# Seven-product FFN up stage: quarter weights formed seven products ahead from four raw tiles, and the down stage's operands in the token forms' space

## The chip, the cores and the metric

One core of one Trainium2 chip runs the whole kernel. The metric is the device time of one execution. The kernel before took 1296.34 us (median of three runs, 1295.82 to 1298.61).

PE is the matrix engine (TensorE), PEld its weight loads, DVE the vector engine, ACT the scalar engine, POOL GpSimd, and SP the engine whose queue issues all DMAs here. Each engine takes its instructions in a fixed order.

## The reference

A transformer block in fp32 on 1024 tokens of width 1024: adaLN modulation, a mixer (attention and a short convolution), a residual with layer norm, and then a convolutional FFN with a second residual and layer norm. The change lies in the FFN:

```
def conv_ffn(h, w_up, ffn_conv_w, ffn_conv_b, w_down):
    u = causal_dwconv(h @ w_up, ffn_conv_w, ffn_conv_b)   # w_up 1024 x 5632, 3 taps along the tokens
    g, val = jnp.split(u, 2, axis=-1)
    return (jax.nn.silu(g) * val) @ w_down                # w_down 2816 x 1024
...
x = layer_norm(DEEPNORM_ALPHA * x + gate_f * ff, ln2_g, ln2_b)
```

## The kernel before

**fp32 from three products.** Every operand is split into a rounded high part (a cast on ACT) and the remainder (a subtract on POOL or DVE). A product is hh + hl + lh, three matmuls of 128x128 by 128x512 each.

**Up stage.** The 2816 columns of each half of `w_up` make 22 pairs i, one gate tile and one value tile of 128 columns. Pairs 0 and 1 are computed plainly (`first_pairs`, L828), while the second half of the tokens is still being made. Pairs 2 to 21 are each a 2x2 block product by seven products (Winograd's form), so one pair takes 7 x 12 = 84 matmuls (`quarter_mm`, L930) where the plain form takes 96. I number a pair's products n = 0 to 6 by their weight quarter: a11, a12, a22, s2, s1, s3, s4. The token side (h2 and its sums T1 to T4) is formed once, by `hsum` (L903) and `hform` (L897, L898). The weight side is formed per pair: four combinations on DVE (L938 to L941) and seven splits `wquarter`, a cast on ACT (L923) and a subtract on POOL (L924). The split quarters go into a ring of eight tiles, `wform`: qb0h, qb0l, qb1h, qb1l, wf0 to wf3.

**Raw weights.** A pair reads two raw tiles of 512 KB (`load_raw`, L766), from a pool of two buffers, so the next pair's loads wait until this pair's quarters are formed.

**Evacuation.** Products land in PSUM (`pw`: two banks for the accumulating products and s3; `p`: p2, p4, p3), and are added up in SBUF tiles cg and cv by ACT copies and DVE adds (L951 to L967). Then come the taps (ACT L834, DVE L836), silu (ACT L860), the product (DVE L861), and a store of 512 KB to DRAM (`acts`, L862).

**Down stage.** Before it starts, the pools of the up stage are closed and new ones opened (L979 on). For each slice i the kernel loads acts[i] and w_down[i] (L1020, L1023), multiplies w_down by the gate row on POOL (L1024) and splits both (L126: casts on ACT; subtracts on DVE for acts, on POOL for w_down). Groups of 2, 4, 4, 4, 4, 4 slices run over eight token tiles, two halves each (L1036), and DVE adds each result to the residual y (L1040). The residual (x1s) is reloaded into y after the token forms have read it (L976).

**What sets the order.** A scheduler fixes each engine's order at build time, from data dependences and its own estimate of durations; the order of the text is only a priority.

```
    for i in range(2, NFF):
        up_pair(i)
        if 2 <= i < 2 + NT:
            SP.dma_start(out=ra[i - 2], in_=x1s[i - 2])
    close(tfp, wup, h2p)
    fp, fpool = pool_("fp", bufs=2)
```

Of the kernel before, what the change touches and what calls it, by code (L numbers as in the profile page):

```python
# [67 lines left out]
def block_kernel(ctx: ExitStack, tc: tile.TileContext, a: dict, out: bass.AP, dbg=None):  # L68
# [1048 lines left out]
```

## Time and profile before

| | us |
|---|---|
| median of the runs | 1296.34 |
| profiled execution, its own time | 1297.43 |
| its span in the trace | 1295.6 |
| PE busy | 1159.7 (90%) |
| DVE / POOL / ACT busy | 876.8 / 677.9 / 536.2 |
| first_pairs ends, seven-product pairs begin | 609.1 |
| last seven-product matmul ends | 1017.3 |
| down stage runs without gaps from | 1043.0 |
| last matmul | 1284 |

The trace's times count from the start of the span. A matmul's listed length (about 0.39 us) overlaps the next one's; the distance from start to start is its price.

### The profile page before, as it was taken

To read this page: it belongs to the slowest core of one execution; us is meant where nothing else is said; L and a number is where in the kernel's file an instruction comes from. 1 tells how busy PE (TensorE), PEld (TensorE's weight loads), DVE (VectorE), ACT (ScalarE), POOL (GpSimd) and SP (SyncE) were. 2 spreads that over 40 slices of the span, in tenths; PEclk is the share of its full clock that TensorE was granted. 3 is DMA by queue.
4 is the path that set the end of the run, shared out by engine and by line. 5 is a ranking of instruction groups with operands and counts; after the bars stand their busy time and mean duration, and the time that the engine had idled before them with its cause. 6 is when DMAs were issued, how large, how long until landed. Compare 5 with 4: busy or idle time off the path is not lost.

```text
span 1295.6 us, 14458 instructions
## 1 busy us (share of the span) xinstructions
PE 1159.7 (90%) x5204; PEld 934.1 (72%) x5204; DVE 876.8 (68%) x1207; ACT 536.2 (41%) x836; POOL 677.9 (52%) x434
## 2 busy tenths in 40 slices
PE   2998978879988989999899999999999389999996
PEld 1766756767867768877688877778778268888885
DVE  6964889867767647679577777777777573543347
ACT  2544323237768723447344444444444342221011
POOL 4666625313538623536655656556566098834226
PEclk9989988889989989999899999999999789999998
DMA  9301454643244133232322212222122364421002
GB/s 376 138 25 49 133 198 156 187 111 80 54 99 130 34 114 114 66 98 99 114 84 79 82 65 83 81 81 82 67 83 79 109 232 131 146 98 51 15 32 99
DMA packets 46219, 134.47 MB, mean 104 GB/s; under 512 B 5452, under 2 KB 15308, under 8 KB 45124
## 3 DMA queue, kind: packets, MB, share of 16 engines
q1 hardware_dynamic: 46148, 133.55, 32.0%
q8 instruction: 41, 0.67, 0.2%
q14 instruction: 30, 0.25, 0.1%
HBM read 100.76 MB, written 19.92 MB: 93 GB/s over the span
## 4 chain that ended last, share of the span: by engine, by line
PE 45%; POOL 16%; DMA 14%; DVE 14%; issue 6%; ACT 3%; SPq 1%; POOLq 0%; DVEq 0%; ACTq 0%
PE pd L1036 16%; DMA ur<-w_up_in 8%; PE pso L704 6%; POOL wf L924 6%; PE pw L930 5%; PE p L930 4%; PE s L594 3%; DMA y<-ada_r_in 3%; PE pu L828 2%; PE tp L628 2%; PE pa L283 2%; POOL qb1l L924 1%; POOL qb0h L924 1%; POOL qb1h L924 1%; POOL qb0l L924 1%
## 5 line engine op out<-in xcount | busy, mean ns | idle before, releaser
L924 POOL TENSOR_TENSOR wf<-ur,wf 128x512 fp32r<-128x512 f32 x68 | 114.0, 1692 | 84.1 <-ACT wf L923 84.1
L1040 DVE TENSOR_TENSOR y<-pd,y 128x512 f32<-128x512 f32 x96 | 61.6, 683 | 104.6 <-PE pd L1036 104.5
L930 PE MATMUL p<-h2h,wf 128*128 128x512 f32 x240 | 81.3, 400 | 3.8 <-POOL wf L924 3.3
L923 ACT CAST wf<-ur 128x512 fp32r<-128x512 f32 x68 | 41.0, 620 | 104.7 <-DMA ur<-w_up_in 76.5
L1024 POOL TENSOR_TENSOR rd<-rd,gate_f 128x1024 f32<-128x1024 f32 x22 | 58.4, 2664 | 49.2 <-DMA rd<-w_down_in 49.2
L283 PE MATMUL psc<-hTh,hwc 128*128 128x512 f32 x192 | 65.1, 407 | 14.7 <-DVE y L528 8.8
L283 PE MATMUL psc<-hTl,hwc 128*128 128x512 f32 x192 | 64.4, 402 | 0.0
L632 DVE TENSOR_TENSOR ptl<-tp,pth 128x512 fp32r<-128x512 f32 (+1 forms) x96 | 50.7, 550 | 20.1 <-ACT pth L631 19.4
L283 PE MATMUL psc<-hTh,lwc 128*128 128x512 f32 x192 | 63.7, 400 | 0.0
L1036 PE MATMUL pd<-h2h 128*128 128x512 f32 x144 | 40.7, 411 | 23.6 <-ACT h2h L123 21.2
L599 DVE TENSOR_REDUCE mx<-s 128x1 f32<-128x128 f32 (+3 forms) x64 | 47.6, 752 | 17.3 <-PE s L594 15.8
L930 PEld LDWEIGHTS p<-h2h,wf 128*128 128x128 f32 x240 | 44.9, 190 | 17.4 <-POOL wf L924 6.8
L283 PEld LDWEIGHTS psc<-hTh,hwc 128*128 128x128 f32 x192 | 37.4, 196 | 24.3 <-issue 11.3
L601 ACT ACTIVATE p<-s,mx 128x128 f32<-128x128 f32 (+3 forms) x64 | 47.8, 748 | 12.7 <-DVE mx L599 12.4
L631 ACT CAST pth<-tp 128x512 fp32r<-128x512 f32 (+1 forms) x96 | 43.7, 485 | 19.0 <-PE tp L628 17.1
L1036 PEld LDWEIGHTS pd<-h2h 128*128 128x128 f32 x144 | 28.4, 199 | 30.7 <-ACT h2h L123 21.6
L628 PE MATMUL tp<-ident,p 128*128 128x128 f32 x288 | 47.9, 276 | 0.7 <-DVE ptl L632 0.6
L930 PE MATMUL p<-h2l,wf 128*128 128x512 f32 x120 | 47.3, 394 | 0.0
L836 DVE SCALAR_TENSOR_TENSOR rbuf<-rbuf,cols,rbuf 128x1023 f32<-128x1023 f32 (+1 forms) x24 | 34.7, 1465 | 18.4 <-ACT rbuf L834 18.4
L283 PEld LDWEIGHTS psc<-hTl,hwc 128*128 128x128 f32 x192 | 37.9, 197 | 8.2
L283 PEld LDWEIGHTS psc<-hTh,lwc 128*128 128x128 f32 x192 | 37.4, 195 | 8.3
L836 DVE SCALAR_TENSOR_TENSOR rbuf<-cu,cols,rbuf 128x1023 f32<-128x1023 f32 (+1 forms) x24 | 37.8, 1593 | 6.7 <-ACT rbuf L834 6.7
(929 smaller groups left out, 3678.1 us busy)
## 6 DMA issues: line engine op xcount, KB each, us to landing
ur<-w_up_in SPq DMA_DIRECT2D x44, 512.0 KB
y<-ada_r_in SPq DMA_DIRECT2D x32, 512.0 KB
ra<-acts SPq DMA_DIRECT2D x22, 512.0 KB
rd<-w_down_in SPq DMA_DIRECT2D x22, 512.0 KB
ada<-ada_m_in SPq DMA_DIRECT2D x8, 1024.0 KB
acts<-rbuf SPq DMA_DIRECT2D x14, 512.0 KB
rwc<-w_conv_in SPq DMA_DIRECT2D x12, 512.0 KB
xn<-x_in SPq DMA_DIRECT2D x8, 512.0 KB
```

The source lines that it names most:

```text
L283: T.matmul(out=ps[hf][0:n_out, :], lhsT=w[:, k, :], rhs=hT[hf][m][:, k, :], start=first and i == 0, stop=last and i == 2)
L599: V.tensor_reduce(out=mx, in_=st[:, 0:n], op=ALU.max, axis=mybir.AxisListType.X, negate=True)
L601: A.activation(out=pt[:, 0:n], in_=st[:, 0:n], func=AF.Exp, bias=mx, accum_out=sm[:, c:c + 1])
L628: T.transpose(tp[:, q4 * P:(q4 + 1) * P], pts[q4][:, kt * P:(kt + 1) * P], ident)
L632: V.tensor_tensor(ptl[:, c0:], tp[:, c0:], f(pth[:, c0:]), op=ALU.subtract)
L704: T.matmul(out=ps[:, hf, :], lhsT=l[:, i, :], rhs=r[:, hf * 512:(hf + 1) * 512], start=part == 1 and i == 0 and n == 0, stop=part == 0 and ...
L836: V.scalar_tensor_tensor(out=u[:, d:n], in0=src[:, 0:n - d], scalar=w(2 - d), in1=u[:, d:n], op0=ALU.mult, op1=ALU.add)
L924: G.tensor_tensor(t[:, 1], s_, f(t[:, 0]), op=ALU.subtract)
L930: T.matmul(out=ps, lhsT=w[:, m, k, :], rhs=b[mb][:, k, :], start=first and k == 0 and n == 0, stop=k == 3 and n == 2, skip_group_check=True)
L1024: G.tensor_tensor(raw, raw, gate_f, op=ALU.mult)
L1036: T.matmul(out=ps[hf], lhsT=l[:, sl], rhs=r[:, hf * 512:(hf + 1) * 512], start=k == 0 and m == 0, stop=k == n - 1 and m == 2)
L1040: V.tensor_tensor(rs_, ps[hf], rs_, op=ALU.add)
```

## The change

Four parts. (1) Raw weights have four tiles: pair i+2 loads into the two that pair i used, as soon as its seventh quarter is formed; the same four tiles later hold acts and w_down. (2) The text forms quarter j+7 before product j. Pairs 2 and 3 start interleaved. (3) p2 and p4 go to single PSUM banks (`o`, `nm`), p4 is copied by ACT and product 3 added by DVE; the cg/cv/u tiles come from a list of five. The token forms are all subtracted on DVE; the gate row is made after pair 5. (4) The down stage's operands live in the tiles of the token forms and quarters, in the order in which pair 21's products free them; its first two slices are loaded and formed inside pair 21.

```
+    raws += [tfpool.tile([P, 1024], F32, name=f"wr{i}") for i in range(2, 4)]
...
-    hform(R[1][1], tforms[1], V)
-    hform(R[1][0], tforms[3], G)
-    hform(R[0][0], tforms[0], V)
-    hform(R[0][1], tforms[2], G)
+    hform(R[1][0], T4, V)
+    hform(R[1][1], T2, V)
+    hform(R[0][0], T1, V)
+    hform(R[0][1], T3, V)
...
+    def wform_of(i, n):
+        rg, rv = rw[i]
+        a11, a12, a21, a22 = rg[:, 0:512], rg[:, 512:1024], rv[:, 0:512], rv[:, 512:1024]
+        if n == 3:
+            V.tensor_tensor(a22, a21, a22, op=ALU.add)
...
+        wq[i, n] = wquarter((a11, a12, a22, a11, a22, a21, a12)[n])
+        if n == 6:
+            pair_raw(i + 2)
...
-            p2 = tptile(f"p2_{i}")
+            p2 = otile(f"p2_{i}")
...
+            p4 = nmtile(f"p4_{i}")
+            quarter_mm(p4, w, T4)
+            A.copy(cv[:, lo], p4)
+        elif n == 3:
+            quarter_mm(al, w, T2, first=False)
+            V.tensor_tensor(cv[:, lo], al, cv[:, lo], op=ALU.add)
...
+    order = [(2, 0), (2, 1), (3, 0), (3, 1)] + [(i, n) for i in (2, 3) for n in range(2, 7)]
+    order += [(i, n) for i in range(4, NFF) for n in range(7)]
...
+    slots = [quarters(b) for b in (B(0, 0), B(1, 0), T4)] + [wform[4:8]] + [quarters(b) for b in (T2, T1, T3, B(1, 1))]
+    slots.append(wform[0:4])
...
+    def ff_load(i):
+        rw["d", i] = load_raw(acts[i]), load_raw(a["w_down"][i])
...
+    for j, (i, n) in enumerate(order):
+        if j + AHEAD < len(order):
+            wform_of(*order[j + AHEAD])
+        if i == NFF - 1 and n == 0:
+            ff_load(0)
+            ff_load(1)
+        product(i, n)
+        if i == NFF - 1 and n < 2:
+            ff_form(n)
+            ff_load(n + 2)
+        if n == 6:
+            leave(i)
...
-    close(tfp, wup, h2p)
-    fp, fpool = pool_("fp", bufs=2)
```

**Order A, DVE at the start of the seven-product pairs.** The tf and h2l rows are remainders of T1 to T4, y the sums, and the rbuf rows taps of first_pairs, which free its PSUM (pu). Before:

```order
L126 TENSOR_TENSOR h2l1_4977<-y_82,h2h1_4976 128x512
L903 TENSOR_TENSOR y_82<-y_82 128x2x512 x2
L898 TENSOR_TENSOR tf1l_5189<-y_82,tf1h_5188 128x1024
L836 SCALAR_TENSOR_TENSOR rbuf0_4978<-pu001_5192,cols_58,rbuf0_4978 128x511
L851 SCALAR_TENSOR_TENSOR rbuf0_4978<-edge0_5010,cols_58,rbuf0_4978 128x1
L836 SCALAR_TENSOR_TENSOR rbuf2_4980<-pu011_5222,cols_58,rbuf2_4980 128x511
```

Now:

```order
L901 TENSOR_TENSOR tf0l_5173<-y_82,tf0h_5172 128x1024 x2
L901 TENSOR_TENSOR tf2l_5177<-y_82,tf2h_5176 128x1024
L126 TENSOR_TENSOR h2l1_4975<-y_82,h2h1_4974 128x512
L901 TENSOR_TENSOR tf2l_5177<-y_82,tf2h_5176 128x1024
L906 TENSOR_TENSOR y_82<-y_82 128x2x512
L901 TENSOR_TENSOR h2l1_4975<-y_82,h2h1_4974 128x1024
L906 TENSOR_TENSOR y_82<-y_82 128x2x512
L901 TENSOR_TENSOR tf1l_5175<-y_82,tf1h_5174 128x1024
L901 TENSOR_TENSOR h2l1_4975<-y_82,h2h1_4974 128x1024
L839 SCALAR_TENSOR_TENSOR rbuf0_4976<-pu001_5178,cols_58,rbuf0_4976 128x511
L854 SCALAR_TENSOR_TENSOR rbuf0_4976<-edge0_5008,cols_58,rbuf0_4976 128x1
```

The remainders of T3 (tf2l) and T4 (h2l1 at 128x1024), which POOL made before, stand ahead of the taps.

**Order B, PE at the hand-over to the down stage.** The pw and p rows are products of pairs 20 and 21, and pd rows matmuls of the down stage (pd010: group 0, token tile 1, half 0). Before:

```order
L930 MATMUL pw21_7785<-tf2l_5191,qb1h_2062 128x512
L930 MATMUL pw21_7785<-tf2h_5190,qb1h_2062 128x512 x2
L930 MATMUL pw21_7785<-tf2l_5191,qb1h_2062 128x512
L930 MATMUL pw21_7785<-tf2h_5190,qb1h_2062 128x512
L1036 MATMUL pd000_7940<-h2h0_4218 128x512
L1036 MATMUL pd001_7941<-h2h0_4218 128x512
L1036 MATMUL pd010_7956<-h2h0_4218 128x512
```

Now:

```order
L941 MATMUL pw20_7622<-tf2h_5176,qb1l_2063 128x512
L941 MATMUL p3_21_7843<-h2h1_4974,qb1l_2063 128x512
L941 MATMUL p3_21_7843<-h2l1_4975,qb1l_2063 128x512
L1091 MATMUL pd000_7866<-h2l0_4219,h2h0_4218 128x512 x3
L941 MATMUL p3_21_7843<-h2h1_4974,qb1l_2063 128x512 x2
L941 MATMUL p3_21_7843<-h2l1_4975,qb1l_2063 128x512
L941 MATMUL p3_21_7843<-h2h1_4974,qb1l_2063 128x512 x2
L941 MATMUL p3_21_7843<-h2l1_4975,qb1l_2063 128x512
L941 MATMUL p3_21_7843<-h2h1_4974,qb1l_2063 128x512 x2
L941 MATMUL p3_21_7843<-h2l1_4975,qb1l_2063 128x512
L941 MATMUL p3_21_7843<-h2h1_4974,qb1l_2063 128x512
L1091 MATMUL pd011_7883<-h2l0_4219,h2h0_4218 128x512 x3
```

Group 0 begins inside pair 21; its slice 0 (pd000, pd011, three matmuls each) stands between that pair's products. The product that reads quarter qb1l of pair 21 (its n = 6) follows directly on pair 20's, which reads the same ring tile (its n = 5).

**Order C, POOL at the hand-over.** gate_f rows multiply w_down by the gate row, L126 rows split the result, and the others are quarters of pairs 20 and 21. Before:

```order
L924 TENSOR_TENSOR qb1h_2062<-ur43_7765,qb1h_2062 128x512
L924 TENSOR_TENSOR qb0h_2060<-ur21_7763,qb0h_2060 128x512
L924 TENSOR_TENSOR qb1l_2063<-ur21_7763,qb1l_2063 128x512
L1024 TENSOR_TENSOR rd0_7926<-rd0_7926,gate_f_5173 128x1024
L1024 TENSOR_TENSOR rd1_7935<-rd1_7935,gate_f_5173 128x1024
L126 TENSOR_TENSOR h2h0_4218<-rd0_7926,h2h0_4218 128x1024
L126 TENSOR_TENSOR h2l0_4219<-rd1_7935,h2l0_4219 128x1024
L1024 TENSOR_TENSOR rd2_8072<-rd2_8072,gate_f_5173 128x1024
L1024 TENSOR_TENSOR rd3_8081<-rd3_8081,gate_f_5173 128x1024
```

Now:

```order
L917 TENSOR_TENSOR wf0_4230<-wr0_4234,wf0_4230 128x512
L1028 TENSOR_TENSOR wr1_4235<-wr1_4235,gate_f_5171 128x1024
L917 TENSOR_TENSOR qb0l_2061<-wr3_5170,qb0l_2061 128x512
L126 TENSOR_TENSOR h2l0_4219<-wr1_4235,h2l0_4219 128x1024
L917 TENSOR_TENSOR qb1h_2062<-wr3_5170,qb1h_2062 128x512
L1028 TENSOR_TENSOR wr1_4235<-wr1_4235,gate_f_5171 128x1024
L1028 TENSOR_TENSOR wr3_5170<-wr3_5170,gate_f_5171 128x1024
L126 TENSOR_TENSOR h2l1_4975<-wr1_4235,h2l1_4975 128x1024
L917 TENSOR_TENSOR qb1l_2063<-wr2_5169,qb1l_2063 128x512
L126 TENSOR_TENSOR h2l0_4219<-wr3_5170,h2l0_4219 128x1024
```

Between pair 21's quarter qb1h (n = 5) and its last, qb1l (n = 6), there now stand two multiplies and a split of the down stage's slices 1 and 2.

## Rows read from the trace of the kernel before

**Rows 1.** The page, the chain that ended last: shares of the span by line.

```profile
PE pd L1036 16%; DMA ur<-w_up_in 8%; PE pso L704 6%; POOL wf L924 6%; PE pw L930 5%; PE p L930 4%; PE s L594 3%; DMA y<-ada_r_in 3%; PE pu L828 2%; PE tp L628 2%; PE pa L283 2%; POOL qb1l L924 1%; POOL qb0h L924 1%; POOL qb1h L924 1%; POOL qb0l L924 1%
```

**Rows 2.** Busy time by stretch: stretch, length, engines in the order named, PEclk, DMA, GB/s.

```profile
651.15:670.38 19.23, 19.23 (x86) 15.77 (x85) 14.42 (x15) 8.50 (x12) 10.24 (x7) 1.00 0.25 83
850.37:870.41 20.04, 19.48 (x84) 15.70 (x84) 15.07 (x15) 8.94 (x13) 11.76 (x7) 1.00 0.23 79
633.82:1017.30 383.48, 375.46 (x1621) 302.29 (x1619) 281.80 (x266) 169.10 (x245) 214.96 (x130) 1.00 0.22 76
1017.30:1043.01 25.71, 2.08 (x5) 1.16 (x4) 11.43 (x11) 8.86 (x9) 8.76 (x4) 0.57 0.52 184
```

**Rows 3.** The chain that ended last, about 850 to 862 us: start, length, what.

```profile
850.37 3.44 DMA ur<-w_up_in
...
854.54 1.30 POOL wf L924
...
857.29 2.28 POOL qb0h L924
...
861.30 3.53 DMA ur<-w_up_in
```

**Rows 4.** The page, costliest groups: the casts of weight quarters on ACT.

```profile
L923 ACT CAST wf<-ur 128x512 fp32r<-128x512 f32 x68 | 41.0, 620 | 104.7 <-DMA ur<-w_up_in 76.5
```

**Rows 5.** Groups of instructions, 712 to 990 us, taps on DVE and ACT.

```profile
L836 DVE SCALAR_TENSOR_TENSOR cu<-rbuf,cols,cu 128x1023 f32<-128x1023 f32 (+1 forms) x16 | 26.6, 1685 | 4.1 <-ACT cu L834 4.1
...
L834 ACT ACTIVATE rbuf<-rbuf,cols 128x1024 f32<-128x1024 f32 x8 | 9.7, 1238 | 0.0
```

**Rows 6.** PE in order of time: start, length, what, [idle before <-releaser].

```profile
611.89 0.47 PE L930 MATMUL pw<-h2h,qb0h 128*128 128x512 f32 x1 [1.51 <-DVE rbuf L836]
...
623.08 0.79 PE L930 MATMUL pw<-tf1h,qb1l 128*128 128x512 f32 x1 [3.60 <-ACT qb1l L923]
```

**Rows 7.** Busy time by stretch, PE alone: stretch, length, PE, PEclk, DMA, GB/s.

```profile
609.10:626.47 17.37, 11.31 (x42) 0.86 0.56 188
626.47:633.82 7.35, 7.35 (x21) 0.63 0.39 135
```

**Rows 8.** DVE in order of time, 606 to 610 us.

```profile
606.35 1.22 DVE L898 TENSOR_TENSOR tf1l<-y,tf1h 128x1024 fp32r<-128x1024 f32 x1
607.92 0.75 DVE L836 SCALAR_TENSOR_TENSOR rbuf<-pu,cols,rbuf 128x511 f32<-128x511 f32 x1 [0.35 <-ACT rbuf L834]
```

**Rows 9.** Busy time by stretch, the matmuls of line 664 alone.

```profile
595.40:598.40 3.00, 1.92 (x16) 1.00 0.00 0
```

**Rows 10.** PE in order of time, 1016 to 1052 us.

```profile
1016.91 0.39 PE L930 MATMUL pw<-tf2h,qb1h 128*128 128x512 f32 x1
1038.48 2.07 PE L1036 MATMUL pd<-h2h 128*128 128x512 f32 x4 [21.18 <-ACT h2h L123]
...
1047.45 2.84 PE L1036 MATMUL pd<-h2l 128*128 128x512 f32 x10
1050.13 0.84 PE L1036 MATMUL pd<-h2h 128*128 128x512 f32 x3
```

**Rows 11.** The chain that ended last, 1027 to 1043 us.

```profile
1027.31 0.32 SPq L862
...
1028.15 5.97 DMA rd<-w_down_in
...
1037.31 3.34 POOL rd L1024
1040.65 2.32 POOL h2h L126
```

**Rows 12.** Groups of instructions, 1040 to 1260 us, POOL.

```profile
L1024 POOL TENSOR_TENSOR rd<-rd,gate_f 128x1024 f32<-128x1024 f32 x21 | 55.3, 2643 | 19.3 <-DMA rd<-w_down_in 19.3
L126 POOL TENSOR_TENSOR ff0dl<-rd,ff0dh 128x1024 fp32r<-128x1024 f32 x3 | 10.2, 3390 | 0.0
...
L126 POOL TENSOR_TENSOR ff4dl<-rd,ff4dh 128x1024 fp32r<-128x1024 f32 x2 | 4.9, 2451 | 16.4 <-ACT ff4dh L123 16.4
```

More of the change, by code (lines that the diff above doesn't have):

```diff
@@ L762, in block_kernel, with load_raw @@
     wform = [t for b in fixed for t in b] + [wupool.tile([P, 1024], F32R, name=f"wf{i}", bufs=1) for i in range(4)]
-    def load_raw(ci):
-        raw = wupool.tile([P, 1024], F32, tag="wraw", name=f"ur{ci}")
-        SP.dma_start(out=raw, in_=a["w_up"][ci])
+    raws = [wupool.tile([P, 1024], F32, name=f"wr{i}", bufs=1) for i in range(2)]
+    raw_ring = cycle(raws)
+    def load_raw(src):
+        raw = next(raw_ring)
+        SP.dma_start(out=raw, in_=src)
         return raw
     def load_up(ci, dst, le=G):
-        raw = load_raw(ci)
+        raw = load_raw(a["w_up"][ci])
         wh, wl = dst
@@ L888, in block_kernel @@
     tforms.append(B(0, 1))
+    T1, T2, T3, T4 = tforms
     first_pairs(1)
-    for i in range(2):
-        gated(i, us[i, 0], us[i, 1])
     def hform(src, dst, eng):
@@ L985, in block_kernel @@
-    slot_ring = cycle(slots)
-    g2, b2_ = [fpool.tile([P, D], F32, name=nm, bufs=1) for nm in ("g2", "b2")]
+        cu_free.extend((cv, cg, uv, ug))
+    ra = [y[:, t, :] for t in range(NT)]
+    order = [(2, 0), (2, 1), (3, 0), (3, 1)] + [(i, n) for i in (2, 3) for n in range(2, 7)]
+    order += [(i, n) for i in range(4, NFF) for n in range(7)]
+    for i in range(2):
+        gated(i, us[i, 0], us[i, 1])
+    pair_raw(2)
+    pair_raw(3)
+    for j in range(4):
+        wform_of(*order[j])
@@ new lines, in block_kernel, with ff_form @@
+    slots.append(wform[0:4])
+    slot_ring = cycle(slots)
+    parts = {}
+    def ff_load(i):
+        rw["d", i] = load_raw(acts[i]), load_raw(a["w_down"][i])
+    def ff_form(i):
+        ah, al, dh, dl = parts[i] = next(slot_ring)
+        rawa, raw = rw["d", i]
+        split(rawa, ah, al, le=V)
+        G.tensor_tensor(raw, raw, gate_f, op=ALU.mult)
+        split(raw, dh, dl)
+    for j, (i, n) in enumerate(order):
[10 more added lines that the diff above has]
+            leave(i)
+            if 4 <= i < 4 + NT:
+                SP.dma_start(out=ra[i - 4], in_=x1s[i - 4])
+            if i == 5:
+                gate_row(gate_f, 3, "gf", tptile)
@@ L1012, in block_kernel @@
         last = gi == len(groups) - 1
-        parts = []
         if last:
@@ L1017, in block_kernel @@
         for i in grp:
-            ah, al, dh, dl = next(slot_ring)
-            rawa = fpool.tile([P, S], F32, tag="ra", name=f"ra{i}")
-            SP.dma_start(out=rawa, in_=acts[i])
-            split(rawa, ah, al, le=V)
-            raw = fpool.tile([P, D], F32, tag="rd", name=f"rd{i}")
-            SP.dma_start(out=raw, in_=a["w_down"][i])
-            G.tensor_tensor(raw, raw, gate_f, op=ALU.mult)
-            split(raw, dh, dl)
-            parts.append((ah, al, dh, dl))
+            if i not in parts:
+                ff_form(i)
+                if i + 2 < NFF:
+                    ff_load(i + 2)
         n = len(grp)
```

110 lines of the change are left out of this document (54 added, 56 removed).

## The prediction

> **What bounds the kernel now.** I read the chain that ended last first. Down-stage matmuls hold its largest share, but next stand the loads of w_up with 8% and the POOL subtracts of quarters with 6% [rows 1]. So the seven-product stage is not held by PE alone. Then I cut that stage by time. An early pair takes 19.23 us with PE busy throughout; a later one takes 20.04, with PE busy 19.48 [rows 2]. The chain inside a later pair runs load, POOL, POOL, load, with no matmul in it [rows 3], and the casts idled 76.5 us for the loads [rows 4]: two raw tiles make each pair's loads wait for the previous pair's last subtract. Third, the hand-over: from the last seven-product matmul at 1017.30 to 1043.01 PE does five matmuls [rows 2], because the chain runs from the store of the last pair through the first loads of the new pools, POOL's two multiplies and a split [rows 11]. Fourth, the start of the stage, where PE idles 1.51 and 3.60 us [rows 6] and then runs at a granted clock of 0.63 over 7.35 us [rows 7]. The down stage itself runs matmul against matmul, three in 0.68 us (1050.13 and the rows behind it) [rows 10], and I expect nothing from it.
>
> **Price of a matmul.** 19.23 us / 84 = 0.229 us in a pair, 0.68 / 3 = 0.227 in the down stage. The change neither adds nor removes one, so all that can be won is waiting. I work from the profiled execution, 1297.43 us (span 1295.6 and 1.8 around it); the median of the runs is 1.1 lower.
>
> **Term 1, the pairs: minus 12.0.** From 633.82 to 1017.30 are 383.48 us [rows 2]. Up to 633.82 there were 42 + 21 = 63 matmuls [rows 7] of 20 x 84 = 1680, so 1617 were left, 19.25 pairs. At 19.23 us they cost 370.2, a loss of 13.3 that four raw tiles should remove: a load of 3.44 to 3.53 us [rows 3] then starts a whole pair ahead. The gate row comes in here, 16 small matmuls in 1.92 us, of which the distances leave some 1.6 [rows 9]; I take 13.3 - 1.3 = 12.0 to leave its copies hidden. What is late next? The evacuation: cv is the same tile in every pair, so ACT's copy of p4 for pair i+1 waits for the taps of pair i. From the end of product (i, 5): two adds of p7, which I estimate at the 0.75 us of a tap of that width [rows 8], 1.5; a scaling of 1.24 on ACT and four taps of 1.69 [rows 5], 8.0; the copy at a cast's 0.62 [rows 4] and an add, 1.4: 10.9 in all. Only then may product (i+1, 4) reuse its bank. PE has five products in between, 5 x 2.75 = 13.7 us, so 3 us of slack. Products (i+1, 4) and (i+1, 5) close the loop at 10.9 + 5.5 = 16.4, under 19.23. Bounds: all of it, 13.3, and half of it, 6, if ACT, blocked at that copy, delays the casts queued behind it.
>
> **Term 2, the start: minus 3.3.** Four more remainders of 1.22 us stand on DVE ahead of the taps [order A, rows 8], 4.9 us in all; against that POOL no longer works beside them, so I put the first tap at 608.6 instead of 607.92. The first two products need the two PSUM pairs of first_pairs, freed by the 5th and the 11th tap operation, and p2 and p4 now need the single banks freed by the 13th and 16th. At 0.75 each [rows 8] these are 612.4, 616.9, 618.4 and 620.6. Behind the second bank the products follow one another: 616.9 + 4 x 2.75 gives 60 matmuls by 627.9, with the clock up. Before had 63 by 633.82; now it would be 86 by then, 5.3 us ahead. If the idle of some 3 us lowers the clock as the 3.60 us did (21 matmuls took 7.35 us instead of 4.8, and some before them), about 4 us go: 1.4 ahead. I take the middle, 3.3; bounds 0 and 7. On SP, eight reloads of x1s and two stores stand ahead of pair 4's loads; these wait for token forms that end by 609 and for gated products near 621, and the quarters then in work have their raw tiles already.
>
> **Term 3, the hand-over: minus 19.3.** Before: group 0 of the down stage is 8 x 2 x 2 x 3 = 96 matmuls. At 1050.13 24 were done (4 from 1038.48, 20 more at the lower clock up to 1047.45 and behind it) [rows 10], so it ends at 1050.13 + 72 x 0.2267 = 1066.45, 49.15 after 1017.30, where 21.76 would do: 27.4 lost. Now slices 0 and 1 are formed inside pair 21, and PE goes from one stage to the other without a gap if POOL keeps up. It does not quite. Pair 21's last quarter takes the ring tile that product (20, 5) reads, and PE wants it right behind [order B]. On POOL two multiplies and a split stand ahead of it [order C]. Count from the end of product (20, 4), which frees the tile of the quarter before: PE does the end of p4, product (21, 3), three pd, product (20, 5), two matmuls on the high part and three pd: 7.7 us. POOL does a cast's wait of 0.62 [rows 4], a subtract of 1.7, two multiplies of 2.64, a split of 2.45 to 3.39 [rows 12], a subtract of 1.3 to 2.28 [rows 3], and waits about a microsecond for two loads: 12.3 to 14.3. PE stalls some 5.1. Then pd011 and product (21, 4) wait for pair 20's taps through the p4 copy, about 1.5. Group 1 needs slice 5, ten multiplies and splits later: 26.4 us at 2.64, 33.9 at 3.39, while PE has 134 matmuls, 30.4 us; I take 1.5. Sum 8.1, and 27.4 - 8.1 = 19.3. Bounds: 27.4 with no stall, and 10 with every POOL operation at 3.39 and a lowered clock after the stalls.
>
> POOL's own rows show the danger: a subtract takes 1.30 us alone and 2.28 where DVE combines weights [rows 3], a split 2.45 or 3.39 [rows 12]. The Trainium skill, GPSIMD Engine Reference, section 1 (Specifications), says that GpSimd shares its SBUF interfaces with VectorE and that they collide when a DVE instruction has two SBUF inputs; by that rule, which these rows agree with, DVE's splits of acts would hold POOL at the higher price through the hand-over, which is the third rival below.
>
> **What costs nothing.** Copy and add change places for p4 and product 3 (same count, same engines). Reading a single PSUM bank for p2 costs nothing while its add ends within a pair. The tail is unchanged: its rows of weights are loaded early into free tiles.
>
> **Sum.** 12.0 + 3.3 + 19.3 = 34.6; 1297.4 - 34.6 = 1262.8, or 1262 against the median.
>
> **Rivals.**
> - *No stall at the hand-over.* POOL gets its loads earlier than I count, and slices come in time: 8.1 more, 1254; with the start at its best, 1250. For it: POOL idles 19.3 us for loads in the down stage [rows 12]. Chance 0.18.
> - *The raws gain nothing.* Four tiles still wait for the last quarter of pair i, and if that quarter is formed late, a pair stays at 20.0: 1262 + 12 = 1274. Against it: a load of 3.5 us has a whole pair of 19 us. Chance 0.05.
> - *POOL binds the hand-over.* All its operations there at 3.39, term 3 gives 10, and the stalls lower the clock: 1271 to 1276. Chance 0.17.
> - *Slower: the evacuation loop binds every pair.* If ACT, stuck at the p4 copy until DVE's taps are through, also holds the copies that PE's next products wait for, the loop of 16.4 gets longer than a pair. To eat the 22.6 us of terms 2 and 3 over 19 pairs it must last 20.0 + 1.2 = 21.2 us, 5 more than I add up; at 22.5 us a pair the time is 1296 - 22.6 + 19 x 2.5 = 1321. For it: one cv tile and one bank for p4. Against it: 3 us of slack and PE's order with five products between. Chance 0.06.
>
> **How the numbers follow.** The forecast, 1255 to 1270, has 0.54. 1250 to 1277 takes in the first three rivals but for their ends, and leaves out slower and some of both tails. Faster by over 0.2% (about what a measurement of this kernel can tell from no change, 2.6 us) holds for all cases but the last, less a rest: 0.92; within 0.2% 0.02; slower 0.06.
>
> **What would show it.** Term 1: a pair at about 19.2 us at its middle and late in the stage alike, and casts that no longer idle for loads. Term 2: the first tap on DVE near 608.6, and 60 products' matmuls by 628 to 632. Term 3: pd matmuls inside pair 21, gaps of some 2 to 6 us ahead of p3 of pair 21, and the last POOL split of slice 5 about when group 1 wants it. The forecast is wrong if pairs take over 19.6 us, if PE idles ahead of product (i+1, 4), or if gaps at the hand-over add up to over 15 us.

## The result: slower by 1.8%

| | before | after |
|---|---|---|
| median of the runs, us | 1296.08 (4 runs, 1295.77 to 1298.61) | 1319.04 (4 runs, 1318.93 to 1320.79) |
| ratio after / before | | 1.0176, 95% interval 1.0158 to 1.0194 |
| profiled execution, its own time, us | 1297.43 | 1318.93 |
| last matmul ends in the trace, us | 1284.2 | 1305.9 |

The forecast was 1262, in a range of 1250 to 1277, with a chance of 0.06 for slower. The 0.06 came.

### The profile page after: what moved, and what is told of

Same layout as the page of the kernel before. It is cut to its first block, busy times and chain, and to the rows that moved or that the text cites. A ratio compares the mean times of both kernels' runs of the same rounds, so it can differ in the third digit from the quotient of the medians.

```text
span 1317.1 us, 14454 instructions
## 1 busy us (share of the span) xinstructions
PE 1165.2 (88%) x5204; PEld 931.1 (71%) x5204; DVE 897.6 (68%) x1211; ACT 539.5 (41%) x836; POOL 659.2 (50%) x430
## 4 chain that ended last, share of the span: by engine, by line
PE 57%; DVE 19%; DMA 7%; ACT 6%; issue 6%; POOL 5%; SPq 1%; POOLq 0%; DVEq 0%; ACTq 0%
PE pd L1091 14%; PE pw L941 13%; PE p L941 7%; PE pso L704 6%; PE s L594 3%; DVE rbuf L839 3%; PE psc L283 3%; PE pu L831 2%; DMA y<-ada_r_in 2%; PE tp L628 2%; PE pa L283 2%; PE o L620 1%; PE o L618 1%; DMA wr<-w_up_in 1%; POOL y L1068 1%
## 5 line engine op out<-in xcount | busy, mean ns | idle before, releaser
L917 POOL TENSOR_TENSOR wf<-wr,wf 128x512 fp32r<-128x512 f32 x68 | 106.0, 1564 | 106.4 <-ACT wf L916 74.2
L1091 PE MATMUL pd<-h2l,h2h 128*128 128x512 f32 x528 | 133.3, 398 | 9.4 <-DVE y L1095 8.3
L1091 PEld LDWEIGHTS pd<-h2l,h2h 128*128 128x128 f32 x528 | 100.7, 192 | 33.9 <-DVE y L1095 10.8
L839 DVE SCALAR_TENSOR_TENSOR rbuf<-rbuf,cols,rbuf 128x1023 f32<-128x1023 f32 (+1 forms) x50 | 88.2, 1785 | 9.4 <-ACT rbuf L837 9.3
L916 ACT CAST wf<-wr 128x512 fp32r<-128x512 f32 x68 | 41.7, 619 | 81.5 <-PE pw L941 50.8
L1028 POOL TENSOR_TENSOR wr<-wr,gate_f 128x1024 f32<-128x1024 f32 x22 | 60.5, 2761 | 26.2 <-DMA wr<-w_down_in 26.1
L601 ACT ACTIVATE p<-s,mx 128x128 f32<-128x128 f32 (+3 forms) x64 | 47.8, 748 | 12.2 <-DVE mx L599 11.9
L126 POOL TENSOR_TENSOR h2l<-wr,h2l 128x1024 fp32r<-128x1024 f32 x11 | 32.5, 2960 | 40.0 <-ACT h2l L123 40.0
L917 POOL TENSOR_TENSOR qb0h<-wr,qb0h 128x512 fp32r<-128x512 f32 x18 | 28.9, 1608 | 46.0 <-ACT qb0h L916 33.1
```

Of the source, the lines that this page charges most:

```text
L601: A.activation(out=pt[:, 0:n], in_=st[:, 0:n], func=AF.Exp, bias=mx, accum_out=sm[:, c:c + 1])
L839: V.scalar_tensor_tensor(out=u[:, d:n], in0=src[:, 0:n - d], scalar=w(2 - d), in1=u[:, d:n], op0=ALU.mult, op1=ALU.add)
L917: G.tensor_tensor(t[:, 1], s_, f(t[:, 0]), op=ALU.subtract)
L1028: G.tensor_tensor(raw, raw, gate_f, op=ALU.mult)
L1091: T.matmul(out=ps[hf], lhsT=l[:, sl], rhs=r[:, hf * 512:(hf + 1) * 512], start=k == 0 and m == 0, stop=k == n - 1 and m == 2)
```

## The profile after

Names first: the casts of quarters are now line 916 and the subtracts 917. In `product`, ACT's copies are lines 958 (n = 0), 966 (n = 2, p4) and 972 (n = 4), DVE's adds 962 (n = 1), 969 (n = 3), 975 and 976 (n = 5) and 980 (n = 6). The taps are 837 (ACT) and 839 (DVE), the sums of weights 930 to 933, the product's matmuls 941, the down stage's 1091, its adds 1095. T1, T2 and T3 are the tiles tf0, tf1 and tf2.

The page of after: the shares of the chain by line, and the casts on ACT.

```profile
PE pd L1091 14%; PE pw L941 13%; PE p L941 7%; PE pso L704 6%; PE s L594 3%; DVE rbuf L839 3%; PE psc L283 3%; PE pu L831 2%; DMA y<-ada_r_in 2%; PE tp L628 2%; PE pa L283 2%; PE o L620 1%; PE o L618 1%; DMA wr<-w_up_in 1%; POOL y L1068 1%
...
L916 ACT CAST wf<-wr 128x512 fp32r<-128x512 f32 x68 | 41.7, 619 | 81.5 <-PE pw L941 50.8
```

The loads of w_up fall from 8% [rows 1] to 1% of the chain, and the casts now idle mostly for PE instead of 76.5 us for loads [rows 4]. So the four raw tiles do what they were to do. DVE's taps are new in the chain.

Busy time by stretch, after; the columns are those of [rows 2].

```profile
863.18:905.89 42.71, 39.69 (x169) 31.16 (x169) 30.85 (x29) 18.41 (x27) 21.84 (x15) 1.00 0.21 74
905.89:948.61 42.72, 39.69 (x169) 31.17 (x169) 30.85 (x29) 18.40 (x27) 21.99 (x15) 1.00 0.21 75
```

Two pairs (168 matmuls) take 42.72 us, the same each time: 21.36 a pair, against 20.04 and the 19.23 that I had counted on [rows 2]. At 0.2273 us a matmul (the price worked out below) 4.5 us of the 42.72 are lost. The period is two pairs, not one, so something alternates. The waits of PE in one period, after:

```profile
863.18 0.50 PE L941 MATMUL pw<-h2h,wf 128*128 128x512 f32 x1 [0.23 <-DVE rbuf L976]
869.58 0.50 PE L941 MATMUL p<-h2h,wf 128*128 128x512 f32 x1 [1.04 <-ACT rbuf L966]
873.42 0.50 PE L941 MATMUL pw<-tf0h,qb0l 128*128 128x512 f32 x1 [0.78 <-DVE rbuf L969]
877.41 0.50 PE L941 MATMUL pw<-tf2h,qb1h 128*128 128x512 f32 x1 [0.97 <-ACT rbuf L972]
905.89 0.50 PE L941 MATMUL pw<-h2h,qb1h 128*128 128x512 f32 x1 [0.23 <-DVE rbuf L976]
```

All four waits lie in the first 14 us of the period; from 877.4 to 905.7 PE runs through. In that slow half (i,5) is followed by (i+2,0), p3 of pair i+1 and p4 of pair i+2, which wants the single bank that ACT's copy has not emptied (1.04); then (i+1,4) waits for the add of product 3 (0.78) and (i+1,5), directly behind it, for the copy of (i+1,4) (0.97). What the copy waited for is in the chain of waits through that half, after (start, length, what):

```profile
861.84 0.69 DVE rbuf L975
862.53 0.61 DVE rbuf L976
...
863.16 1.25 ACT rbuf L837
...
865.78 0.68 DVE wr L930
866.46 0.67 DVE cu L839
...
867.58 1.28 DVE rbuf L839
868.86 1.68 DVE wr L931
...
872.69 0.69 DVE rbuf L969
```

From the end of (i,5) at 861.8 to the end of the add at 873.4 are 11.6 us, with two sums of weights on DVE between the taps. I had added up 10.9. ACT and DVE near the end of that path, after:

```profile
868.77 1.76 DVE L931 TENSOR_TENSOR wr<-wr,wr 128x512 f32<-128x512 f32 x1
868.95 0.58 ACT L966 COPY rbuf<-p 128x512 f32<-128x512 f32 x1
...
870.45 2.32 DVE L839 SCALAR_TENSOR_TENSOR cu<-rbuf,cols,cu 128x1022 f32<-128x1022 f32 x1
```

So the path has two parts. The first 7.7 us, up to the end of the copy at 869.5, lead through the one cv tile: adds, scaling and the two taps of the value half (with a sum and a tap of the gate half between them). For this copy PE waits 1.04 us. The other 3.8 us are DVE's queue: the add of product 3 stands there behind the sum 931 and a tap of the gate half. Beside POOL's subtracts these two took 1.76 and 2.32 us, where a sum and a tap of the same shapes took 0.68 (at 865.78) and 1.28 (at 867.58); 2.1 of the 11.6 us are this slowing.

The start of the stage, after: PE's only wait, and PE by stretch up to the time at which before had done 63 matmuls [rows 7].

```profile
611.78 0.56 PE L941 MATMUL pw<-h2h,qb0h 128*128 128x512 f32 x1 [4.34 <-DVE rbuf L839]
```

```profile
609.10:633.82 24.72, 22.04 (x89) 0.93 0.40 151
```

One wait of 4.34 us in place of 1.51 and 3.60 [rows 6], a mean clock of 0.93, and 89 matmuls instead of 63. 26 x 0.229 = 5.9 us ahead.

The hand-over, after: PE's waits from 1029 us on.

```profile
1034.78 0.50 PE L941 MATMUL p<-h2h,qb1l 128*128 128x512 f32 x1 [2.59 <-ACT qb1l L916]
...
1040.05 1.22 PE L941 MATMUL p<-h2h,qb1l 128*128 128x512 f32 x2 [2.19 <-POOL qb1l L917]
1045.11 1.14 PE L1091 MATMUL pd<-h2l,h2h 128*128 128x512 f32 x3 [0.42 <-ACT rbuf L966]
1048.35 0.50 PE L941 MATMUL pw<-tf0h,qb0l 128*128 128x512 f32 x1 [2.10 <-DVE rbuf L969]
1074.62 2.93 PE L1091 MATMUL pd<-h2l,h2h 128*128 128x512 f32 x6 [5.99 <-DVE y L1095]
...
1089.36 0.95 PE L1091 MATMUL pd<-h2l,h2h 128*128 128x512 f32 x3 [1.02 <-DVE y L1095]
```

The one wait of 21.18 us [rows 10] is gone, and ten small ones, 16.9 us together, stand in its place. From 1028 to 1082 the mean granted clock is 0.81 (PE by stretch):

```profile
1028.00:1082.00 54.00, 38.16 (x129) 0.81 0.55 183
```

The largest wait, 5.99, is for DVE's adds, which empty the banks. DVE in order of time, after:

```profile
1041.00 3.38 DVE L839 SCALAR_TENSOR_TENSOR rbuf<-rbuf,cols,rbuf 128x1022 f32<-128x1022 f32 x1
...
1047.62 0.68 DVE L969 TENSOR_TENSOR rbuf<-pw,rbuf 128x512 f32<-128x512 f32 x1
1048.22 2.81 DVE L126 TENSOR_TENSOR h2h<-wr,h2h 128x1024 fp32r<-128x1024 f32 x1
...
1064.98 5.71 DVE L839 SCALAR_TENSOR_TENSOR rbuf<-rbuf,cols,rbuf 128x1023 f32<-128x1023 f32 x2
1070.61 3.36 DVE L126 TENSOR_TENSOR tf0h<-wr,tf0h 128x1024 fp32r<-128x1024 f32 x1
1073.88 0.68 DVE L1095 TENSOR_TENSOR y<-pd,y 128x512 f32<-128x512 f32 x1
```

Taps and remainders of 2.8 to 3.4 us stand in front of adds of 0.68 in one queue.

**Where the time went.** Put a price of 0.2273 us (100 us for 440, p4two below) on each matmul that a window shows. From 633.82 to 1000 us before did 1551, a loss of 366.18 - 352.5 = 13.6; after did 1434 and, in 2.1 us by their listed lengths (1.6 by the distances), the 16 small ones of the gate row, which moved into this stretch: 366.18 - 326.0 - 2.1 = 38.1. From 1000 us to the last matmul before lost 27.8 and after 29.5. So the pairs lost 24.5 us more, the gate row costs 2.1, the hand-over lost 1.7 more, and the start gave 5.9: 22.4, against 21.5 between the two profiled executions (a few matmuls are uncertain in such counts).

## The experiments

Each kernel was timed beside the kernel before. The two losses are counted as above, in the profiled execution: "pairs" from 633.82 to 1000 us, without the gate row (2.1 us, in cu6p4 and cu6p4s 2.3), and "hand-over" from 1000 us to the last matmul.

| kernel | median, us | ratio to before (95%) | pairs | hand-over |
|---|---|---|---|---|
| before | 1296 | | 13.6 | 27.8 |
| after | 1319.0 | 1.0176 (1.0158 to 1.0194) | 38.1 | 29.5 |
| cu6 | 1285.5 | 0.9914 (0.9887 to 0.9940) | 8.1 | 23.8 |
| cu6r3 | 1275.2 | 0.9837 (0.9808 to 0.9866) | 4.5 | 18.5 |
| p4two | 1290.8 | 0.9959 (0.9944 to 0.9973) | 13.4 | 26.7 |
| part1 | 1327.1 | 1.0243 (1.0204 to 1.0283) | 36.5 | 38.3 |
| sumsG | 1355.1 | 1.0453 (1.0430 to 1.0476) | 66.5 | 34.7 |
| cu6p4 | 1304.5 | 1.0061 (1.0029 to 1.0093) | 26.1 | 25.7 |
| cu6p4s | 1301.8 | 1.0033 (1.0015 to 1.0052) | 27.0 | 24.7 |
| cu6s | 1288.3 | 0.9936 (0.9915 to 0.9957) | 10.2 | 23.8 |
| cu6noal | 1278.7 | 0.9858 (0.9830 to 0.9886) | 8.1 | 17.6 |
| cu6nomult | 1282.1 | 0.9884 (0.9855 to 0.9915) | 7.2 | 19.2 |
| cu6notap | 1282.8 | 0.9893 (0.9868 to 0.9917) | 8.1 | 20.4 |
| r3fix | 1275.0 | 0.9828 (0.9796 to 0.9860) | 6.1 | 16.8 |
| r3ok | 1284.0 | 0.9904 (0.9878 to 0.9930) | 3.4 | 31.0 |
| r3ok2 | 1276.5 | 0.9847 (0.9817 to 0.9878) | 4.3 | 20.2 |
| r3ok3 | 1279.2 | 0.9867 (0.9846 to 0.9889) | 4.7 | 22.2 |
| r3lean | 1267.4 | 0.9767 (0.9724 to 0.9810) | 3.8 | 11.6 |

Two readings need care. cu6r3 and r3fix load into tiles that are still to be read, so they do not compute the reference's result, and cu6noal, cu6nomult, cu6notap and r3lean leave work out: their times say only what a wait or a piece of work is worth. And the losses belong to the profiled execution, which in r3ok took 1288.7, 4.7 us more than the median, and in cu6p4s 1306.1, 4.3 more.

**The pairs: the tile, the bank, the order.** Three edits of the changed kernel, each by itself.

```
-    cu_free = [tfpool.tile([P, S], F32, name="cu4")] + rbuf
+    cu_free = [tfpool.tile([P, S], F32, name=f"cu{i}") for i in (4, 5)] + rbuf    # cu6, cu6r3
...
+    ones = prpool.tile([P, P], F32R, name="ones")                                 # cu6, and bd
...
-    raws += [tfpool.tile([P, 1024], F32, name=f"wr{i}") for i in range(2, 4)]     # cu6r3
+    raws += [tfpool.tile([P, 1024], F32, name=f"wr{i}") for i in range(2, 3)]
...
-            p2 = otile(f"p2_{i}")                                                 # p4two
+            p2 = tptile(f"p2_{i}")
-            p4 = nmtile(f"p4_{i}")
+            p4 = (nmtile if i % 2 else otile)(f"p4_{i}")
```

cu6: 

> A sixth tile for the evacuation (cu4 and cu5; room for it from the two constant tiles ones and bd, moved out of the constants' pool), so that cv is another tile in each pair. Theory A (the evacuation path through the one cv tile): ACT's copy of p4 no longer waits for the taps of the pair before, the pairs go from 21.36 to about 19.3 us, and 19.25 pairs x 2.05 = 39 us go: about 1280. Rival B (the path is long anyway, because DVE's taps and weight sums collide with POOL's subtracts): a pair stays above 20.5 us, and the time above 1300. Rival C (the order in which PE takes the products decides, whatever the tiles): pairs near 21.3 and 1315 to 1320.

cu6r3: 

> The same space, shared out another way: six evacuation tiles and three raw tiles instead of five and four. Theory A: most of what the sixth tile gives stays; with three raw tiles one of a pair's two loads of 3.5 us again waits for the last subtract of the pair before, so a pair lies between 19.3 and the 20.04 that the kernel before had with two: 1280 to 1295. If raw tiles are what counts: 20 us a pair or more and above 1293. Rivals B and C as for cu6: above 1300.

p4two: 

> Five evacuation tiles as in the changed kernel, but p4 alternates between the two single banks and p2 shares the pair of banks with p3. The copy of p4 still waits for the taps through the one cv tile, but the scheduler now puts four products of 2.75 us between (i,5) and (i+1,4) in every pair (11.0 us), where the changed kernel has three (8.2) and five (13.7) in turn. Theory A (path of 11.5 us from (i,5) to the add behind product 3, against the products between): 0.5 to 1 us of gap a pair, pairs at about 19.9 and 1319 - 19.25 x 1.46 = 1291. Rival B (path itself above a pair): no gain, 1315 to 1320. Rival D (it is the bank of p4 alone): no gap at all, 19.3 and 1280.

A sixth tile takes 34 us away (5 less than A's number), the second bank for p4 28. PE in p4two by stretch:

```profile
700.00:800.00 100.00, 99.92 (x441) 1.00 0.23 81
800.00:900.00 100.00, 100.00 (x439) 1.00 0.24 84
```

440 matmuls in 100 us are 19.1 us a pair, with the one cv tile kept: not even the gap of 0.5 to 1 us that I expected shows. So the path of 11.6 us is harmless where the products between are spread evenly and p4 finds a bank.

Each edit also changed the order in which PE takes the products, so the order has to be counted too. Between (i,5) and (i+1,4) stand, from 800 to 985 us, 39 and 57 matmuls in turn in after, 7 to 11 and 59 to 63 in cu6, 35 and 41 in r3ok (below; six tiles and one bank for p4), and 48 each time in p4two. In after PE waits 2.05 to 2.10 us in all there, each time that only 39 stand between. In cu6 and r3ok it waits nothing in the shorter half, though that is shorter still. So the tile alone is enough, and C (PE's order whatever the tiles) falls; so does B (collisions alone), since DVE and POOL do the same work in these kernels. In p4two order and bank changed together, and which of the two was enough there stays open. The 1291 of p4two came out, but not for the reason given: its pairs are faster than expected, and it loses 4 us at the stage's beginning (waits of 1.45, 1.46 and 1.10 us up to 697) and 4.2 at its end (0.92 and 3.31 us, at 991.8 and 998.8).

**The down stage as it was.** The pairs of after, then the pools and loops of before.

```
+    close(tfp, wup, h2p)
+    fp, fpool = pool_("fp", bufs=2)
...
```

part1: 

> The pairs of the changed kernel with the down stage of the kernel before (own pools, slices formed behind the last pair). Says what the hand-over is worth. By the traces the hand-over lost 27.4 us before and about 25 after, and the down stage behind group 0 took 229.2 before and 231.8 after: theory A, the hand-over gave nothing, 1316 to 1323. Rival: it did give the 19 us that I had put down for it and the pairs lost more than I count: 1338.

8 us slower than after, between the two numbers: the shared space is worth 8, not 19. Of the 38.3 us that part1 loses behind 1000 us, 11.6 go before its last product ends at 1047.8 (159 matmuls in 47.8 us): the ends of these pairs, which in before lost 0.9 (72 matmuls in 17.3 us). Behind that product the old hand-over costs what it cost: waits of 20.33 and 2.46 us, against 21.18 and 2.46 in before.

**The sums of weights on POOL.**

```
-            V.tensor_tensor(a22, a21, a22, op=ALU.add)
+            G.tensor_tensor(a22, a21, a22, op=ALU.add)
...
```

sumsG: 

> The changed kernel (five evacuation tiles, one bank for p4) with the four sums of a pair's weights on POOL instead of DVE. In the slow half of two pairs 0.7 and 1.7 us of them stand between DVE's taps, in the path of 11.5 us from (i,5) to the add behind product 3; the scheduler now also puts four products between in each pair. Theory A: path 9.1 us against 11.0, no gap, pairs at 19.3 and 1280; if the order counts for nothing, a gap of 1 us in two pairs, 1297. Rival B (taps beside POOL's operations cost 2.3 us instead of 1.3, and POOL now has eleven of them a pair): pairs above 20.5, 1305 or more.

36 us slower than after: theory A's number was wrong by 75. The taps' mean rises from 1785 to 2001 ns, 0.9 us for a pair's four, so B's collision is there but is not most of it. The chain of waits of sumsG shows the rest:

```profile
849.26 1.28 POOL wr L931
850.55 2.23 POOL wf L917
...
852.85 1.27 POOL wr L932
...
854.67 0.61 ACT qb1l L916
855.28 0.49 ACT rbuf L972
```

The quarter's cast waits for a sum on POOL, and the copy that PE needs (972) stands behind that cast on ACT. PE then waits 3.36 us. The path has only been led through another queue.

**Tile and bank together, and the hand-over's loads.**

cu6p4: 

> cu6 and p4two together: six evacuation tiles, and two banks for p4. From 633.82 to 1000 us cu6 did 1587 matmuls and p4two 1564, of some 1612 that fit at 0.227 us. Theory A: with neither the tile nor the bank held, PE is never late in the pairs, about 1605 matmuls, 4 us less than cu6: 1281. The hand-over stays as in cu6 (waits of 6.4 us ahead of p3 of pair 21, 5.4 and 2.7 ahead of group 0). Rival (in cu6 the pairs are no longer what is lost): 1285, as cu6.

cu6p4s: 

> cu6p4 with the down stage's first loads dealt out to other raw tiles: slice 1 follows slice 0 in wr0 and wr1, slice 2 takes wr3 and wr2 behind pair 21's last quarter. In the changed kernel slice 1's tile of acts is the one that pair 21's last quarter is formed from, so its load waits for that subtract, and ACT's cast of that quarter stands behind casts of slices that wait for POOL's multiplies. Theory E (the hand-over is a question of which tile a load waits for): the waits of 6.4, 5.4 and 2.7 us that cu6 shows go, 12 to 15 us less than cu6p4, 1266 to 1270. Rival F (DVE and POOL, colliding at 2.8 to 3.4 us an operation, are what binds the hand-over): the wait only changes its name, at most 4 us less than cu6p4.

```
         if i == NFF - 1 and n == 0:          # cu6p4s, and cu6s on cu6
             ff_load(0)
-            ff_load(1)
...
+        if i == NFF - 1 and n == 0:
+            raw_ring = cycle(raws)
+            ff_load(1)
+        if i == NFF - 1 and n == 3:
+            raw_ring = cycle([raws[3], raws[2], raws[0], raws[1]])
+            ff_load(2)
+            ff_load(3)
```

A miss: each cure works, both together lose 26.1 us in the pairs. cu6p4 does 441 matmuls between 700 and 800 us and 774 in the next 200 (21.7 us a pair), with 1.7 to 1.9 us of wait for line 972 once a pair. Its chain of waits:

```profile
908.77 1.29 POOL qb1l L917
...
910.09 1.78 DVE wr L930
...
912.59 0.60 DVE rbuf L975
...
922.49 1.21 DVE cu L839
...
923.78 1.06 ACT cu L863
924.83 0.51 ACT wf L916
925.34 0.49 ACT rbuf L972
```

No cv tile and no bank in it. DVE's sum 930 waits 3.8 us at the head of its queue for POOL's subtract, with the adds 975 and 976 behind it. So the taps are late, ACT's silu (863) waits 6.0 us for them, and the copy for PE stands behind the silu. What the chains of after, sumsG and cu6p4 share is a path over POOL, DVE and ACT to PE that the order within the queues makes; which link is late differs from one order to the next. No run fixed the order and changed tile and bank alone, so why both cures together undo each other is read from this chain and not tested. cu6p4s says little on the hand-over, since its pairs were bound the same way.

cu6s: 

> cu6 (which keeps PE busy in the pairs) with slice 1 loaded behind slice 0 into wr0 and wr1, and slice 2 into wr3 and wr2. Theory E (the hand-over waits for loads into the tile that pair 21's last quarter is formed from): the waits of 6.4, 5.4 and 2.7 us go, 1271 to 1274. Rival F (DVE and POOL bind the hand-over): 1281 or more, with longer waits for DVE's adds (y) in their place.

The hand-over loses 23.8 us, as in cu6: the waits for the quarter go from 6.4 to 2.2 us, and those for DVE's adds rise from 2.4 to 8.5. Theory E falls here, F stands.

**Work taken away at the hand-over.**

```
-        split(rawa, ah, al, le=V)
+        if i < 6:                                               # cu6noal
+            A.copy(ah, rawa)
+            parts[i] = ah, ah, dh, dl
+        else:
+            split(rawa, ah, al, le=V)
...
+        if i > 5:                                               # cu6nomult
             G.tensor_tensor(raw, raw, gate_f, op=ALU.mult)
...
-        for d in (1, 2):                                        # cu6notap
+        for d in () if ci % NFF == NFF - 1 else (1, 2):
```

cu6noal: 

> cu6 without DVE's remainders of the first six slices of acts (they are left out, and the high part is read in their place), six operations of 1.2 to 3.1 us in the hand-over. Rival F (DVE, slowed by POOL, binds the hand-over): of the 23.4 us that cu6 loses behind 1000 us 8 to 12 go, 1274 to 1278. Theory E (loads and tiles): at most 2 us, 1283 to 1286.

cu6nomult: 

> cu6 without POOL's multiplies by the gate row for the first six slices (left out), six operations of 2.7 to 3.4 us. Theory F1 (POOL's share of the hand-over binds: the quarter, multiplies and splits stand in one queue, and they slow DVE's taps): of cu6's 23.4 us lost behind 1000 us 10 to 14 go, 1271 to 1276. Theory F2 (DVE's own work binds, whoever runs beside it): at most 4 us, 1281 to 1285.

cu6notap: 

> cu6 without DVE's four taps of pair 21 (left out, ACT's scaling alone stays): four operations of 1.3 to 2.8 us in the last part of the hand-over. Theory F2 (DVE's work binds): 5 to 8 us less, 1277 to 1280. Theory F1 (POOL binds) or E (loads): at most 3 us, 1282 to 1286.

The hand-over's loss falls by 6.2, 4.6 and 3.4 us. The first is near F's number; the other two fall short of the numbers of F1 and F2, and by their times alone they can't be told from cu6. No single one holds it.

**Three raw tiles.**

```
         if i < NFF:                                             # r3fix
-            rw[i] = load_raw(a["w_up"][i]), load_raw(a["w_up"][NFF + i])
+            if i not in rw:
+                rw[i] = [load_raw(a["w_up"][i])]
+            rw[i].append(load_raw(a["w_up"][NFF + i]))
+        if i + 1 < NFF:
+            rw[i + 1] = [load_raw(a["w_up"][i + 1])]
...
+            raw_ring = cycle([raws[1], raws[0], raws[2], cu_free.pop(-2), cu_free.pop()])    # r3ok
...
+            raw_ring = cycle([raws[1], raws[0], cu_free.pop(-2), raws[2], cu_free.pop()])    # r3ok2
...
+            w0, w1, w2 = raws                                                                # r3ok3
+            raw_ring = chain((w1, w0), cycle((w1, w2, cu_free.pop(-2), cu_free.pop(), w0)))
```

r3fix: 

> cu6r3 again with its loads in an order that three raw tiles allow (the second half of pair i+1 and the first half of pair i+2 are loaded behind pair i's last quarter; in cu6r3 the load for pair i+1 overwrote the tile from which pair i's first quarters are formed, so its output was not the reference's). Theory A: a load of 3.5 us has three quarters' time, 8 us, so nothing changes: 1273 to 1279, pairs at 19.1. Rival (three raw tiles bring the load wait back): pairs at 19.5 to 20, 1285 or more.

r3ok: 

> Six evacuation tiles and three raw tiles as in r3fix, with the down stage's loads dealt to five tiles (the three and two free evacuation tiles). In cu6r3 and r3fix the load of slice 1's weights overwrote slice 0's acts, so their outputs were not the reference's, and a wait may have been missing there. Theory A (the pairs need a free cv tile, and a load of 3.5 us has time): pairs at 19.1 as in r3fix, 1270 to 1278. Rival (r3fix gained from the missing wait at the hand-over): 1282 to 1288, like cu6.

r3ok2: 

> r3ok with slice 1's weights loaded into wr2 and its acts into the evacuation tile that pair 20's store frees, instead of the other way round. POOL's multiply for slice 1 now stands third instead of fourth among the multiplies, behind pair 21's last quarter. Theory E' (order of loads and queues, now that the pairs run free): the 10 us wait for slice 1's low part shrinks to 3 or less, 1275 to 1279. Theory F (DVE and POOL, whatever the order): the wait changes its name, 1282 to 1286.

r3ok3: 

> r3ok with slice 1's acts loaded into wr1 behind slice 0's, and its weights into wr2 behind pair 21's last quarter; slice 2 takes the two free evacuation tiles. On POOL pair 21's last quarter and slices 0 and 1 now stand ahead of every other slice, and on ACT too. Theory E': no wait over 4 us at the hand-over, 1268 to 1274. Theory F: waits for DVE's adds and for the splits of 8 us or more together, 1278 to 1284.

PE in r3ok by stretch:

```profile
800.00:900.00 100.00, 100.00 (x439) 1.00 0.22 80
900.00:1000.00 100.00, 100.00 (x439) 1.00 0.23 84
```

The pairs are settled: 3.4 us lost, one wait of 1.0 us in the whole stretch, and a load of 3.5 us needs no fourth tile. r3fix came out in the range of its theory A, but with a tile overwritten. Without that, r3ok came out as the rival had it, at 1284, since it loses 31.0 at the hand-over, 10.0 of it waiting for slice 1's low part. r3ok2 changes only which tile that slice is loaded into and is 7.5 us faster, as E' said, so it was the order of the loads more than a missing wait; r3ok3, tidier by its order, stays 5 us short of E' and shows F's waits, 13.1 us for DVE's adds. So both hold: loads out of order cost 7.5 us by the medians (11 by the two profiled executions), and once they are in order DVE's queue is what is left. DVE in r3ok3, and POOL beside it:

```profile
1000.13 3.41 DVE L839 SCALAR_TENSOR_TENSOR rbuf<-rbuf,cols,rbuf 128x1022 f32<-128x1022 f32 x1
1003.47 3.40 DVE L839 SCALAR_TENSOR_TENSOR rbuf<-cu,cols,rbuf 128x1022 f32<-128x1022 f32 x1
1006.78 3.40 DVE L126 TENSOR_TENSOR wf<-wr,wf 128x1024 fp32r<-128x1024 f32 x1
1010.11 3.37 DVE L864 TENSOR_TENSOR rbuf<-rbuf,rbuf 128x1024 f32<-128x1024 f32 x1
...
1005.74 3.36 POOL L126 TENSOR_TENSOR h2l<-wr,h2l 128x1024 fp32r<-128x1024 f32 x1
1009.05 3.34 POOL L126 TENSOR_TENSOR wf<-wr,wf 128x1024 fp32r<-128x1024 f32 x1
```

POOL runs from 999.86 to 1012.4 without a pause beside them. The last run takes that work away:

```
-        split(rawa, ah, al, le=V)
-        G.tensor_tensor(raw, raw, gate_f, op=ALU.mult)
+        if i < 6:                                               # r3lean, on r3ok3
+            A.copy(ah, rawa)
+            parts[i] = ah, ah, dh, dl
+        else:
+            split(rawa, ah, al, le=V)
+            G.tensor_tensor(raw, raw, gate_f, op=ALU.mult)
```

r3lean: 

> r3ok3 without DVE's remainders of acts and without POOL's multiplies by the gate row for the first six slices (left out; the high part of acts is read in place of the remainder). Theory F (DVE, slowed by POOL, binds the hand-over once pairs and loads are in order): the 13.1 us of waits for DVE's adds go to 3 or less, and 10 to 13 us of the time, 1266 to 1270. Rival (PE waits for pair 21's own evacuation, whoever is busy): at most 4 us, 1275 or more.

11.8 us less than r3ok3. The waits of PE at the hand-over of r3lean (in total, times, longest):

```profile
PE pd L1101 <- DVE y L1105: 3.3, 3, 2.0
PE pd L1101 <- POOL h2l L126: 2.9, 1, 2.9
```

That is F's number: in this order DVE's and POOL's work on the first six slices is what keeps the hand-over from being free. How much of it is DVE's and how much POOL's, this run does not say, and for after itself the same cause is read from its waits and not tested. Of the kernels that leave nothing out and overwrite nothing still to be read, r3ok2 is the fastest of those run: 1276.5, ratio 0.9847 (0.9817 to 0.9878), faster than before and after. r3ok3's interval overlaps with it.

## Why the prediction was wrong

**The bounds of the profile** were read rightly: loads of w_up and POOL's subtracts held the pairs, and the load wait went as forecast.

**Term 1 failed, at one step:** "PE has five products in between, 5 x 2.75 = 13.7 us, so 3 us of slack." I had read the order of one pair and taken it for all. In every second one three products stand between, 8.2 us, and one of them is p4 of pair i+2, which needs the very bank that the copy has to empty. The path I put at 10.9 took 11.6, though not by the sum I gave: the copy needs two taps and not four, and the add needs DVE's queue. Against 13.7 us of products it is nothing; against the 39 matmuls that stand there every second time, 8.9 us, it is 2.7 too long. That is the three waits of 0.23, 1.04 and 0.78 us and slower steps beside them; the fourth wait, 0.97, is for the copy of (i+1,4) directly behind, which my sum did not have. Forecast -12.0 up to 1017 us, measured +24.5 and 2.1 for the gate row up to 1000. The size was near for a kernel whose pairs run free: r3ok brings the 13.6 down to 3.4 and pays the 2.1, which is -8.1.

**The slower rival** named the tile and the bank, and missed the engine. ACT held nothing up at the copy: a cast runs ahead of it from 868.40, the copy starts as the tap ends (868.95 and 868.86), and behind it ACT idles until 872.86. It is the add that stands in DVE's queue. Its 1321, for 22.5 us a pair, is near the 1319 by luck: at the 21.36 that pairs took, its formula gives 1299, and the other 20 us are the hand-over, which gave nothing. What I held against it, the five products, was the step that I had not checked over a second pair.

**Term 2** was right in its mechanism and too small: the first tap on DVE starts at 608.53 (forecast 608.6), 89 matmuls are done by 633.82 where I had 86 with the clock up. I took -3.3, the middle; it was -5.9, within the bounds of 0 to 7.

**Term 3 failed, at its list of stalls.** The first two are near the forecast: 2.59 + 2.19 = 4.8 us ahead of p3 of pair 21 (5.1), 0.42 + 2.10 = 2.5 at pd011 and (21,4) (1.5). The third, 1.5 for group 1, left DVE out: I bounded POOL and let DVE's queue be free, and it held pair 21's taps, the remainders of acts and the adds that empty the banks. 5.99 + 0.37 + 0.88 + 1.02 = 8.3 us of waits, and with the mean clock at 0.81 some 9 us of slower matmuls from 1028 to 1082 (54 us less 29.3 for 129 matmuls less 15.9 of waits). Forecast -19.3; measured +1.7 against before, and -8 against the old hand-over behind the same pairs (part1). The third rival, POOL at its higher price throughout, named the collision; what it hit was DVE.

**The costs put at nothing:** the edit "copy and add change places for p4 and product 3 (same count, same engines)" counted operations and not what they wait for. In after PE's p4 waits for that copy and (i+1,4) for that add; what the edit costs by itself no run shows, since none takes it back alone.

**The signs.** All three that I had named as showing the forecast wrong came: pairs of 21.36 us, a wait ahead of (i+1,4), and gaps of 16.9 us at the hand-over.

## What to carry to other kernels

Slack against PE's order must be counted over the whole period of the order, at its worst place: a schedule written by a program may repeat every two tiles, and a mean over them hides the half that waits. Where a change moves work to ready it earlier, bound every queue that the work passes, and what stands behind it there, before calling the stretch free: an engine at 70% busy can still be the last one for one wait in each period. When one cure helps and another helps, both together need not: look at which queue's head waits now.

## What the runs showed of the hardware

- DVE's operations with two SBUF inputs are slowed by POOL, as POOL's are by DVE [rows 3, 12], and by a larger factor. The remainder of 128x1024 took 1.22 us at 606.35 of before [rows 8] and 3.36 in after at 1070.61; the tap of 128x1022 1.28 (after, 867.58) and 3.38 (1041.00). The adds of 128x512 with one input in PSUM took 0.68 beside POOL too (1073.88; the down stage's 96 have a mean of 683 ns). The Trainium skill, GPSIMD Engine Reference, section 1 (Specifications), names two SBUF inputs of a DVE instruction as a condition for contention on the shared SBUF interfaces. The runs agree; for the size, 2.7 times, only the rows stand.
- Side by side in r3ok3 the two engines gain almost nothing over taking turns. DVE's operations of 128x1022 and 128x1024 start 3.31 and 3.33 us apart (1003.47, 1006.78, 1010.11), and POOL's of 128x1024 start 3.31 apart (1005.74, 1009.05). One DVE operation of that width took 1.22 us at 606.35 of before [rows 8], with POOL idle, and one of POOL's 2.36 beside adds from PSUM (r3ok3, 1013.71): 3.58 one after the other, 3.3 side by side.
- A sum of 128x512 on POOL has a mean of 2.03, 1.81 and 1.54 us for lines 930 to 932 in sumsG, against 0.84, 1.39 and 1.00 for the same lines on DVE in after: moving work off a full queue made each operation longer and put another link into the path.
